# A hybrid decoder block on one core: another order at the start, decay rows stored from ScalarE's queue, and six of the scan's x projections in matmuls of 512 columns

## The chip, the cores and the metric

The kernel runs on one core of a Trainium2 chip. The metric is the device time of one execution in microseconds (us), as a median over runs; lower is better. A profiled execution gives the span from its first to its last instruction, and what each engine did in it: TensorE (PE for matmuls, PEld for loading their stationary operand), VectorE (DVE), ScalarE (ACT), GpSimd (POOL), and SyncE (SP), which here only issues DMAs. SBUF is the on-chip memory; PSUM is the small one into which matmuls accumulate, in banks of 2 KB per partition; 256 tokens of float32 for two column halves fill one bank.

## The reference

One decoder layer, 256 tokens, width 1024, float32. What matters here:

```
proj = rmsnorm(x) @ w_in          # columns: z, xBC, dt, q, k, v, gates
xbc  = silu(causal_dwconv(xBC))   # depthwise, width 4; gives x (2048), B and C (8 groups x 128)
dt   = softplus(dt_raw + bias)    # 32 heads
y    = ssd_scan(x*dt, dt*A, B, C) # chunks of 128; decays exp(cumsum differences)
y    = rmsnorm_by_group((y + x*d) * silu(z)) * w
att  = moba_attention(rope(q), rope(k), v)   # 256 tokens: one causal block
x    = x + (g_ssd*(y@w_ssd) + g_att*(att@w_att)) @ w_out
out  = rmsnorm(x + convffn(rmsnorm(x)))
```

## The kernel before, in words

**Number format.** Every float32 operand of a large matmul is split into a high and a low part (`split_half`: ScalarE copies 128 x 1024 weights into the high part, L107; VectorE subtracts it from the weights, L115). A product is then three matmuls: high by high, high weights by low activations, low weights by high activations. The activations stand as pairs `hn[k]`, high in `[:, 0]` and low in `[:, 1]`, for eight blocks k of 128 input channels.

**Units.** All weights are read in the order of one list (`seq`), 1 MB at a time, through three buffers by SP's queue; `next_unit` loads three units ahead and splits one unit ahead, through four buffers for high halves and four for low ones. A unit of `w_in` is 1024 x 256. `mm_unit` multiplies it in 48 matmuls of 256 columns (L176 to L178), block by block, into one PSUM bank. `mm_wide` uses the pair as one right-hand side of 512 columns (L187: high weights by both parts), then 256 columns for the low weights (L191), into two banks; the part that fell into the second half of each bank is then copied out by ScalarE and added by VectorE.

**Order.** TensorE's order is written by hand. From L302 to L387, the start, the order of ScalarE and VectorE is written by hand too; later a planner orders those two and POOL from the program's order, its own costs and a few `issue_after` marks. Each engine runs its queue strictly in that order, so an instruction that waits holds those behind it.

**The start.** x (transposed) and the first v weights arrive in five pieces (`HEAD`); VectorE weighs x by the norm's weight (L313), ScalarE squares it (L323), TensorE multiplies the raw x for v (L309) and sums the squares (L332). The reciprocal root of the mean comes from ScalarE's Sqrt and VectorE's reciprocal with one Newton step (L339 to L344), is broadcast by a matmul (L260), and multiplies the weighed x (`normed`, L355). The first unit, B and C of group 0, takes its first four blocks as plain float32 (L366, 16 matmuls), since these need no split; its other four go through `mm_unit`.

**The scan, groups g = 0 to 7.** Each group runs `u_bc` (B and C), `u_x`, small matmuls of earlier groups (`small_1`: the scan's output L568, attention scores L608 and outputs L666), `u_qk`, then by turns `u_v`, `u_z`, `u_gate`. `small_2` has the chunk product `s_cb` (L509), the transposes of x (`s_xt`, L537; in groups 2, 4 and 6 by a DMA) and the mean of the gated norm. `conv_silu` runs the width-4 conv: ScalarE starts an accumulator (L398), VectorE adds three shifted products (L402), ScalarE takes a tanh, VectorE multiplies (L406). `u_x` leaves x in its PSUM bank and `u_qk` runs its conv later, straight from the bank, behind the split of the next unit. Four banks go round for all of these (`mm_tile`, tag "mm").

**Decay rows.** `dt_chain` makes dt on small tiles, `dt_sums` the cumulative sums (L705), `dt_turn` transposes them, copies them to SBUF (L716) and stores them to DRAM by POOL's queue (L717). `load_acs(g)` reads four rows back, broadcast to all partitions (L430, POOL's queue); from them ScalarE makes the decays `mx` (L522 to L525), which VectorE multiplies by the chunk product (L527).

**The end.** The down projection's last columns are finished in two token halves: `finished(c, cut)` scales columns up to `cut` on ScalarE and the others on VectorE, and stores both.

Of the kernel before, what the change touches and what calls it, by code (L numbers as in the profile page):

```python
# [19 lines left out]
P = 128  # L20
# [17 lines left out]
C_ID = 256  # L38

HEAD = [0] + [KD + 512 * k for k in (1, 2, 4, 6, 8)]  # L40
# [8 lines left out]
def block_kernel(tc, xtok_d, head_d, par_d, nf_d, con_d, rope_d, win_d, wgate_d, bg_d, watt_d, wssd_d, wout_d, wup_d, wdn_d, out_d):  # L49
# [3 lines left out]
    with st:  # L53
# [11 lines left out]
        con = const.tile([P, C_ID + 7 * P + NH], F32, name="con")  # L65
# [5 lines left out]
        con3 = con[:, C_ID : C_ID + 7 * P].rearrange("p (a b) -> p a b", b=P)  # L71
        ident = con3[:, 0, :]
        mmask = con3[:, 1:4, :]
        amask = con3[:, 4:7, :]
        tri = con3[:, 1, :]
        sel = con[:, C_ID + 7 * P :]
# [5 lines left out]
        nc.scalar.activation(one1, ones[:, 0:1], AF.Sqrt)  # L82
# [73 lines left out]

        def mm_unit(ps, halves, act, first=True, last=True, k0=0, apart=False):


            tiles = [(hi, lo, kk) for hi, lo, n in halves for kk in range(n)]  # L160
            nk = len(tiles)
            km = [(k, m) for k in range(nk) for m in range(2)]
            if apart:
                km.sort(key=lambda x: x[1])
                ps = [p[:, 0, :] for p in ps]
            else:
                ps = [ps[:, m, :] for m in range(2)]
            with tc.manual_schedule(engines=PE_ONLY):
                for k, m in km:
                    hi, lo, kk = tiles[k]  # L170
                    xh, xl = act[k0 + k][:, 0, :], act[k0 + k][:, 1, :]
                    wh = hi[:, kk, m * P : m * P + P]
                    wl = lo[:, kk, m * P : m * P + P]
                    a = first and k == 0 and (m == 0 or apart)
                    z = last and k == nk - 1 and (m == 1 or apart)
                    nc.tensor.matmul(ps[m], wh, xh, start=a, stop=False)  # L176
                    nc.tensor.matmul(ps[m], wh, xl, start=False, stop=False)  # L177
                    nc.tensor.matmul(ps[m], wl, xh, start=False, stop=z)  # L178

        def mm_wide(ps, halves, act, k0=0, nk=KD):  # L180


            tiles = [(hi, lo, kk) for hi, lo, n in halves for kk in range(n)]
            with tc.manual_schedule(engines=PE_ONLY):
                for k, (hi, lo, kk) in enumerate(tiles, k0):
                    for m in range(2):
                        nc.tensor.matmul(flat(ps[m]), hi[:, kk, m * P : m * P + P], flat(act[k]), start=(k == 0),  # L187
                                         stop=False)
                for k, (hi, lo, kk) in enumerate(tiles, k0):
                    for m in range(2):  # L190
                        nc.tensor.matmul(ps[m][:, 1], lo[:, kk, m * P : m * P + P], act[k][:, 0, :], start=False,  # L191
                                         stop=(k == nk - 1))

# [94 lines left out]
        nc.sync.dma_start(con[:, 0 : C_ID + P], con_d[:, 0 : C_ID + P])  # L288
# [3 lines left out]
        nc.sync.dma_start(con[:, C_ID + P :], con_d[:, C_ID + P :])  # L292
        nc.sync.dma_start(rope, rope_d)
        eps = const.tile([P, 1], F32, name="eps")
        n1 = work.tile([P, 4, 2], F32, name="n1")
        rstd1 = n1[:, 3]
# [6 lines left out]
        with tc.manual_schedule(engines=IN_ORDER):  # L303
# [14 lines left out]
            for k in range(2):  # L318
                nc.scalar.activation(sq[:, k], xk[k], AF.Square)
                weigh(k)  # L320
            add(0, 1)
            for k in range(2, KD, 2):
# [8 lines left out]
            for c in range(2):  # L331
                nc.tensor.matmul(stat[:, 0, c : c + 1], sq[:, 0, c * P : c * P + P], ones[:, 0:1], start=(c == 0),  # L332
                                 stop=(c == 1))
            for c in range(2):
                v_raw(6, c)
            v_raw(7, 0)

            mh, root, rr = n1[:, 0], n1[:, 1], n1[:, 2]
            nc.scalar.activation(root, stat[:, 0, 0:2], AF.Sqrt, scale=1.0 / D, bias=eps)  # L339
            nc.vector.tensor_scalar(mh, stat[:, 0, 0:2], -0.5 / D, -0.5 * EPS, op0=ALU.mult, op1=ALU.add)  # L340
            nc.vector.reciprocal(root, root)
# [3 lines left out]
            half0 = split_half(raws[0], 4, 4)  # L345
            rb1 = rms_bcast(rstd1)
            v_raw(7, 1)
            for k in range(KD):
                j = NH * (k % 4)
                nc.tensor.matmul(ps_dt[j : j + NH, 0, :], wdt[:, k], xw[:, k], start=(k < 4), stop=(k >= KD - 4))  # L350

# [11 lines left out]
            for k in range(4):  # L363
                normed(k)
                for m in range(2):
                    nc.tensor.matmul(psbc[:, m], raws[0][:, k, m * P : m * P + P], hnf[k], start=(k == 0 and m == 0),  # L366
                                     stop=False)
            for k in range(4, KD):
                normed(k)
                high(k)  # L370
            for k in range(4, KD):
                low(k)
            nc.scalar.activation(dtp, ps_dt[:, 0, :], AF.Copy)
# [3 lines left out]
            mm_unit(psbc, [half0], hn, first=False, k0=4)  # L377
# [303 lines left out]
        def dt_chain():  # L681
# [18 lines left out]
            nc.vector.tensor_scalar(nega, nega, -1.0, None, op0=ALU.mult)  # L700
            nc.vector.tensor_tensor(r3(3), dt, b3(nega), op=ALU.mult)

        def dt_sums():
# [3 lines left out]
            with tc.high_priority():  # L707
                nc.vector.tensor_copy(flat(acs), ps_a[:, 0, 0 : 2 * NH])
                nc.vector.tensor_tensor(alm, ps_a[:, 0, 2 * NH : 3 * NH], acs[:, 0, :], op=ALU.subtract)

        def dt_turn():
# [3 lines left out]
            with tc.high_priority():  # L715
                nc.scalar.activation(acsT, ps_t[0:NH, 0, :], AF.Copy)  # L716
                nc.gpsimd.dma_start(acsT_d, acsT)  # L717
# [51 lines left out]
        for g in range(NG):  # L769
# [12 lines left out]
            if g % 2 == 0:  # L782
                cols = slice(256 * g, 256 * g + 512)
                for c in range(2):
                    tc.keep_in_program_order(nc.gpsimd.dma_start(gates[:, c, cols], bg_d[cols].partition_broadcast(P)))
# [214 lines left out]
        def finished(c, cut):  # L1000
            lo, hi = xo[:, c, 0:cut], xo[:, c, cut:]
            nc.vector.tensor_scalar(hi, hi, rstd3[:, c : c + 1], None, op0=ALU.mult)
            nc.sync.dma_start(out_d[:, c, cut:], hi)
            nc.scalar.activation(lo, lo, AF.Identity, scale=rstd3[:, c : c + 1])
            (nc.scalar if c else nc.sync).dma_start(out_d[:, c, 0:cut], lo)
# [17 lines left out]
        with tc.manual_schedule(engines=IN_ORDER):  # L1023
# [17 lines left out]
            finished(0, 512)  # L1041
# [10 lines left out]
            finished(1, 352)  # L1052


def _layout(i):
# [48 lines left out]
    con = np.stack([np.eye(P, dtype=np.float32), tri, np.ones((P, P), np.float32), tri, neg, np.zeros((P, P), np.float32), neg], axis=1)  # L1104
# [5 lines left out]
    con = np.concatenate([wdt, con.reshape(P, 7 * P), np.tile(np.eye(NH, dtype=np.float32), (4, 1))], axis=1)  # L1110
# [42 lines left out]
```

## Time and profile before

| | us |
|---|---|
| median of 3 runs | 584.55 (583.65 to 589.18) |
| the profiled execution, its time | 585.26 |
| its span | 583.5 |
| TensorE busy | 572.4 |
| VectorE busy | 457.8 |
| ScalarE busy | 394.8 |
| POOL busy | 66.3 |

Rows of the profile are read so: a row of the timeline has the start in us, the duration in us, engine, line of the kernel, operation, the tiles written and read, and in brackets the engine's idle time before it with what ended that. "x8" are eight of a kind in a row. A row of the chain has start, duration and what. A row of groups has the count, then busy us, the mean in ns of one, the idle time before. A row of DMA issues has KB and the median us from issue to landing. A row of stretches has, for each engine, the busy time and the count, in the order PE, PEld, DVE, ACT, POOL, then clock, share of the DMA engines and GB/s. A row of waits has the total in us, how many, and the longest. A matmul's row is longer than the distance to the next one's start, since matmuls overlap.

### The profile page before, as it was taken

What the parts mean: (1) busy time and instruction counts of PE and PEld (TensorE: products, weight loads), DVE (VectorE), ACT (ScalarE), POOL (GpSimd) and SP (SyncE); (2) the same over time, 40 slices, a digit from 0 to 9 for tenths busy, and PEclk for the clock granted to TensorE, in tenths of its full rate; (3) what the DMA queues carried; (4) which work ended last, traced back from release to release, by engine and by line L of the source; (5) the groups of instructions that cost most, each with busy time, mean ns of one, the idle gap of its engine ahead of it and who ended that gap; (6) DMA issues with size and microseconds to landing.
All of it is one profiled execution on the core that took longest, in us unless ns stands there. A gap on an engine that the chain in (4) does not pass through costs nothing.

```text
span 583.5 us, 9394 instructions
## 1 busy us (share of the span) xinstructions
PE 572.4 (98%) x3510; PEld 502.4 (86%) x3510; DVE 457.8 (78%) x819; ACT 394.8 (68%) x711; POOL 66.3 (11%) x105
## 2 busy tenths in 40 slices
PE   8999989999999999999999999999999999999995
PEld 6899888898988989889888888889888888888884
DVE  4995899889699996998985556768888898884543
ACT  3854698887798777887884344466776767774432
POOL 1001032221223113230121000000000000000200
PEclk9999999999999999999999999999999999999999
DMA  8846556875658946779456756454546555464611
GB/s 304 307 164 244 201 162 210 231 210 188 221 162 195 290 136 220 176 206 292 122 162 240 227 191 214 161 203 144 182 180 216 199 172 206 143 216 155 226 56 72
DMA packets 32845, 113.90 MB, mean 195 GB/s; under 512 B 16880, under 2 KB 17264, under 8 KB 21152
## 3 DMA queue, kind: packets, MB, share of 16 engines
q1 hardware_dynamic: 29632, 104.04, 54.3%
q0 software_dynamic: 2736, 7.51, 4.9%
q10 hardware_dynamic: 432, 1.75, 0.7%
q8 instruction: 27, 0.44, 0.3%
q14 instruction: 18, 0.15, 0.1%
HBM read 108.15 MB, written 1.09 MB: 187 GB/s over the span
## 4 chain that ended last, share of the span: by engine, by line
PE 89%; DMA 3%; DVE 2%; ACT 2%; issue 2%; SPq 0%; POOL 0%; DVEq 0%; ACTq 0%; POOLq 0%
PE up L187 13%; PE mm L208 10%; PE mm L209 10%; PE mm L210 10%; PE mm L187 8%; PE up L191 7%; PE mm L176 6%; PE mm L177 5%; PE mm L178 5%; PE mm L191 4%; PE py L568 2%; DMA raw<-in_win_dram 2%; DMA acsB<-acsT_d 1%; PE po L666 1%; DVE lo L115 1%
## 5 line engine op out<-in xcount | busy, mean ns | idle before, releaser
L115 DVE TENSOR_TENSOR lo<-raw,hi 128x1024 fp32r<-128x1024 f32 x183 | 223.2, 1227 | 69.8 <-ACT hi L107 68.8
L107 ACT ACTIVATE hi<-raw 128x1024 fp32r<-128x1024 f32 x183 | 191.1, 1055 | 105.7 <-PE mm L210 56.3
L176 PE MATMUL mm<-hn,hi 128*128 128x256 f32 x280 | 79.6, 284 | 0.0
L178 PE MATMUL mm<-hn,lo 128*128 128x256 f32 x280 | 79.3, 283 | 0.0
L177 PE MATMUL mm<-hn,hi 128*128 128x256 f32 x280 | 79.2, 283 | 0.0
L187 PE MATMUL up<-xw,hi 128*128 128x512 f32 x320 | 76.3, 391 | 0.0
L187 PEld LDWEIGHTS up<-xw,hi 128*128 128x128 f32 x320 | 58.8, 188 | 11.4
L187 PE MATMUL mm<-hn,hi 128*128 128x512 f32 x224 | 56.8, 395 | 0.0
L177 PEld LDWEIGHTS mm<-hn,hi 128*128 128x128 f32 x280 | 53.7, 192 | 0.2
L176 PEld LDWEIGHTS mm<-hn,hi 128*128 128x128 f32 x280 | 53.7, 192 | 0.2
L178 PEld LDWEIGHTS mm<-hn,lo 128*128 128x128 f32 x280 | 53.7, 192 | 0.1
L402 DVE SCALAR_TENSOR_TENSOR cacc<-mm,par,cacc 128x255 f32<-128x255 f32 (+2 forms) x96 | 44.4, 473 | 3.9 <-ACT cacc L398 3.0
L187 PEld LDWEIGHTS mm<-hn,hi 128*128 128x128 f32 x224 | 40.2, 189 | 8.4 <-issue 1.2
L191 PEld LDWEIGHTS up<-xw,lo 128*128 128x128 f32 x320 | 41.0, 191 | 1.6
L191 PE MATMUL up<-xw,lo 128*128 128x256 f32 x320 | 41.5, 283 | 0.0
L209 PE MATMUL mm<-lo,act 128*128 128x512 f32 (+1 forms) x92 | 35.0, 380 | 0.0
L208 PE MATMUL mm<-hi,act 128*128 128x512 f32 (+1 forms) x92 | 34.9, 380 | 0.0
L210 PE MATMUL mm<-hi,act 128*128 128x512 f32 (+1 forms) x92 | 34.9, 380 | 0.0
L978 POOL TENSOR_TENSOR mt<-x,nfb 128x512 f32<-128x512 f32 x3 | 4.8, 1598 | 258.9 <-DVE x L972 237.6
L191 PEld LDWEIGHTS mm<-hn,lo 128*128 128x128 f32 x224 | 30.6, 190 | 2.2
L191 PE MATMUL mm<-hn,lo 128*128 128x256 f32 x224 | 31.2, 282 | 0.0
L956 DVE SCALAR_TENSOR_TENSOR facc<-ab,par,facc 128x255 f32<-128x255 f32 (+1 forms) x44 | 21.3, 483 | 11.3 <-ACT facc L954 10.6
(226 smaller groups left out, 1130.6 us busy)
## 6 DMA issues: line engine op xcount, KB each, us to landing
raw<-in_win_dram SPq DMA_DIRECT2D x34, 1024.0 KB, 5.9
raw<-in_wup_dram SPq DMA_DIRECT2D x22, 1024.0 KB, 4.8
raw<-in_wdn_dram SPq DMA_DIRECT2D x10, 1024.0 KB, 4.9
raw<-in_wgate_dram SPq DMA_DIRECT2D x8, 1024.0 KB, 5.6
raw<-in_wssd_dram SPq DMA_DIRECT2D x8, 1024.0 KB, 5.1
acsB<-acsT_d POOLq DMA_DIRECT2D x8, 512.0 KB, 5.3
raw<-in_watt_dram SPq DMA_DIRECT2D x4, 1024.0 KB, 5.3
raw<-in_wout_dram SPq DMA_DIRECT2D x4, 1024.0 KB, 5.3
```

The costliest lines, as they stand in the source:

```text
L107: split_half.hi = nc.scalar.activation(hi[:, :n], raw[:, k0 : k0 + n], AF.Copy)
L115: split_half.lo = nc.vector.tensor_tensor(lo[:, :n], raw[:, k0 : k0 + n], hi[:, :n].bitcast(F32), op=ALU.subtract)
L176: nc.tensor.matmul(ps[m], wh, xh, start=a, stop=False)
L177: nc.tensor.matmul(ps[m], wh, xl, start=False, stop=False)
L178: nc.tensor.matmul(ps[m], wl, xh, start=False, stop=z)
L187: nc.tensor.matmul(flat(ps[m]), hi[:, kk, m * P : m * P + P], flat(act[k]), start=(k == 0), stop=False)
L191: nc.tensor.matmul(ps[m][:, 1], lo[:, kk, m * P : m * P + P], act[k][:, 0, :], start=False, stop=(k == nk - 1))
L208: nc.tensor.matmul(o, xh, wh, start=(k == 0 if apart else k0 + k == 0), stop=False)
L209: nc.tensor.matmul(o, xh, wl, start=False, stop=False)
L210: nc.tensor.matmul(o, xl, wh, start=False, stop=(k0 + k == nk - 1))
L402: nc.vector.scalar_tensor_tensor(acc[:, s:], src[:, m, : T - s], w(m, 3 - s), acc[:, s:], op0=ALU.mult, op1=ALU.add)
L956: nc.vector.scalar_tensor_tensor(acc[:, s:], src[:, : T - s], w(2 - s), acc[:, s:], op0=ALU.mult, op1=ALU.add)
```

## The change

- **Start.** x arrives in six pieces (the third is halved) and its first four blocks are squared one at a time; the sums stand before the last raw v product; Abs_reciprocal_sqrt replaces Sqrt and reciprocal; ScalarE's high half of the first unit's second part comes before the broadcast, VectorE's low half only behind the normed rows; the 16 matmuls for dt stand ahead of the broadcast. `mm_passes` runs a unit in passes over all blocks (high by high; low weights by high; high by low for the first unit; both high products, then the low weights, for x of group 0).
- **Small work.** The scalings of `par` and the copy of `acs` go from VectorE to ScalarE; the negation of `nega` is fused; the constants are laid out anew; the loads of the gates' bias (POOL's queue) wait for the start's last split.
- **Decay rows.** Stored by ScalarE's queue.
- **x of groups 2 to 7.** `mm_halves`: for each column half, eight matmuls of 512 columns with the high weights, then eight of 256 with the low weights, into a bank of its own; `joined` copies the second half of each bank out (ScalarE) and adds the first (VectorE) into `xs`; the conv then reads and writes `xs` in SBUF.
- **End.** The second token half in three pieces and three stores.

```diff
-HEAD = [0] + [KD + 512 * k for k in (1, 2, 4, 6, 8)]
+HEAD = [0] + [KD + 512 * k for k in (1, 2, 3, 4, 6, 8)]
...
+        def mm_passes(ps, halves, act, passes, first=True, k0=0):
+            tiles = [(w, kk) for *w, n in halves for kk in range(n)]
+            jobs = [(w, x, k, m) for ws in passes for k in range(len(tiles)) for w, x in ws for m in range(2)]
+            with tc.manual_schedule(engines=PE_ONLY):
+                for i, (w, x, k, m) in enumerate(jobs):
+                    wt, kk = tiles[k]
+                    nc.tensor.matmul(ps[:, m, :], wt[w][:, kk, m * P : m * P + P], act[k0 + k][:, x, :],
+                                     start=first and i == 0, stop=i == len(jobs) - 1)
...
+        def mm_halves(ps, halves, act):
+            tiles = [(hi, lo, kk) for hi, lo, n in halves for kk in range(n)]
+            with tc.manual_schedule(engines=PE_ONLY):
+                for m in range(2):
+                    for k, (hi, lo, kk) in enumerate(tiles):
+                        nc.tensor.matmul(flat(ps[m]), hi[:, kk, m * P : m * P + P], flat(act[k]), start=(k == 0),
+                                         stop=False)
+                    for k, (hi, lo, kk) in enumerate(tiles):
+                        nc.tensor.matmul(ps[m][:, 1], lo[:, kk, m * P : m * P + P], act[k][:, 0, :], start=False,
+                                         stop=(k == KD - 1))
+
+        def joined(dst, ps):
+            for m in range(2):
+                nc.scalar.activation(dst[:, m], ps[m][:, 1], AF.Copy)
+                nc.vector.tensor_tensor(dst[:, m], ps[m][:, 0], dst[:, m], op=ALU.add)
...
-            for k in range(6):
+            for k in range(KD):
                 for c in range(2):
+                    if k == KD - 1 and c:
+                        stats()
                     v_raw(k, c)
...
-            nc.scalar.activation(root, stat[:, 0, 0:2], AF.Sqrt, scale=1.0 / D, bias=eps)
+            nc.scalar.activation(root, stat[:, 0, 0:2], AF.Abs_reciprocal_sqrt, scale=1.0 / D, bias=eps)
-            nc.vector.reciprocal(root, root)
...
-            half0 = split_half(raws[0], 4, 4)
-            rb1 = rms_bcast(rstd1)
-            v_raw(7, 1)
+            hi0 = split_high(raws[0], 4, 4)
             for k in range(KD):
                 j = NH * (k % 4)
                 nc.tensor.matmul(ps_dt[j : j + NH, 0, :], wdt[:, k], xw[:, k], start=(k < 4), stop=(k >= KD - 4))
+            rb1 = rms_bcast(rstd1)
...
+            half0 = split_half(raws[0], 4, 4, hi0)
             for k in range(4, KD):
                 low(k)
...
-            mm_unit(psbc, [half0], hn, first=False, k0=4)
+            mm_passes(psbc, [half0], hn, ([(0, 0)], [(1, 0)], [(0, 1)]), first=False, k0=4)
...
-        with tc.issue_after(hn_end[1]):
+        with tc.issue_after(hn_end[0]):
             for a, b in ((C_NW, C_D), (C_CW, C_FW)):
-                nc.vector.tensor_scalar(par[:, a:b], par[:, a:b], 0.5, None, op0=ALU.mult)
+                nc.scalar.activation(par[:, a:b], par[:, a:b], AF.Copy, scale=0.5)
...
         def u_x(g):
             hv = next_unit()
-            ps = mm_tile()
-            mm_unit(ps, hv, hn)
             xs = S[g]["xs"] = ssp.tile([P, 2, T], F32, tag="xs", bufs=2, name="xs")
-            S[g]["x_ps"] = ps
+            if g > 1:
+                ps = [mm_tile(), mm_tile()]
+                mm_halves(ps, hv, hn)
+                joined(xs, ps)
+                S[g]["x_ps"] = xs
+                return
+            ps = S[g]["x_ps"] = mm_tile()
+            if g:
+                mm_unit(ps, hv, hn)
+            else:
+                mm_passes(ps, hv, hn, ([(0, 0), (0, 1)], [(1, 0)]))
...
-                nc.vector.tensor_copy(flat(acs), ps_a[:, 0, 0 : 2 * NH])
+                nc.scalar.activation(flat(acs), ps_a[:, 0, 0 : 2 * NH], AF.Copy)
...
-                nc.gpsimd.dma_start(acsT_d, acsT)
+                nc.scalar.dma_start(acsT_d, acsT)
...
-                    tc.keep_in_program_order(nc.gpsimd.dma_start(gates[:, c, cols], bg_d[cols].partition_broadcast(P)))
+                    with tc.issue_after(hn_end[1]):
+                        bg = nc.gpsimd.dma_start(gates[:, c, cols], bg_d[cols].partition_broadcast(P))
+                    tc.keep_in_program_order(bg)
...
-            finished(1, 352)
+            finished(1, (0, 256, 640, 1024))
```

More of the change, by code (lines that the diff above doesn't have):

```diff
@@ L64, in block_kernel @@
         par = const.tile([P, NPAR], F32, name="par")
-        con = const.tile([P, C_ID + 7 * P + NH], F32, name="con")
+        con = const.tile([P, C_MASK + 6 * P], F32, name="con")
         rope = const.tile([P, 2, T], F32, name="rope")
@@ L70, in block_kernel @@
         wdt = con[:, 0:C_ID].rearrange("p (k h) -> p k h", h=NH)
[L71 to L76, printed above, removed]
+        ident = con[:, C_ID:C_SEL]
+        sel = con[:, C_SEL:C_MASK]
+        masks = con[:, C_MASK:].rearrange("p (a b) -> p a b", b=P)
+        mmask = masks[:, 0:3, :]
+        amask = masks[:, 3:6, :]
+        tri = masks[:, 0, :]
         ones = const.tile([P, P], F32, name="ones")
@@ L287, in block_kernel @@
             nc.sync.dma_start(head[:, a:b], head_d[P * a : P * b].rearrange("(p n) -> p n", p=P))
-        nc.sync.dma_start(con[:, 0 : C_ID + P], con_d[:, 0 : C_ID + P])
+        nc.sync.dma_start(con[:, 0:C_MASK], con_d[:, 0:C_MASK])
         load_to(1)
@@ L291, in block_kernel @@
         load_to(2)
-        nc.sync.dma_start(con[:, C_ID + P :], con_d[:, C_ID + P :])
+        nc.sync.dma_start(con[:, C_MASK:], con_d[:, C_MASK:])
         nc.sync.dma_start(rope, rope_d)
         eps = const.tile([P, 1], F32, name="eps")
-        n1 = work.tile([P, 4, 2], F32, name="n1")
-        rstd1 = n1[:, 3]
+        mh, root, rr, rstd1 = (work.tile([P, 2], F32, name=n) for n in ("n1mh", "n1r", "n1rr", "rstd1"))
         vt0 = ssp.tile([P, 2, T], F32, tag="vt", bufs=2, name="vt")
@@ L316, in add, with stats @@
                 nc.vector.tensor_tensor(sq[:, a], sq[:, a], sq[:, b], op=ALU.add)
-            for k in range(2):
+            def stats():
+                for c in range(2):
+                    nc.tensor.matmul(stat[:, 0, c : c + 1], sq[:, 0, c * P : c * P + P], ones[:, 0:1], start=(c == 0),
+                                     stop=(c == 1))
+            for k in range(4):
                 nc.scalar.activation(sq[:, k], xk[k], AF.Square)
                 weigh(k)
-            add(0, 1)
-            for k in range(2, KD, 2):
+                if k:
+                    add(0, k)
+            for k in range(4, KD, 2):
                 nc.scalar.activation(sq[:, k : k + 2], chan[:, k : k + 2, 0], AF.Square)
@@ L367, in block_kernel @@
                                      stop=False)
+            nc.scalar.activation(dtp, ps_dt[:, 0, :], AF.Copy)
             for k in range(4, KD):
@@ L699, in dt_chain @@
                 nc.scalar.activation(nega, par[:, C_AL : C_AL + NH], AF.Exp)
-            nc.vector.tensor_scalar(nega, nega, -1.0, None, op0=ALU.mult)
-            nc.vector.tensor_tensor(r3(3), dt, b3(nega), op=ALU.mult)
+            nc.vector.scalar_tensor_tensor(r3(3), dt, -1.0, b3(nega), op0=ALU.mult, op1=ALU.mult)
         def dt_sums():
@@ L998, in rstd_3, with finished @@
             nc.vector.scalar_tensor_tensor(rstd3[:, c : c + 1], h, 1.5, r, op0=ALU.add, op1=ALU.mult)
[L1000 to L1005, printed above, removed]
+        def finished(c, cuts):
+            for i, (a, b) in enumerate(zip(cuts, cuts[1:])):
+                x, r = xo[:, c, a:b], rstd3[:, c : c + 1]
+                if i:
+                    nc.vector.tensor_scalar(x, x, r, None, op0=ALU.mult)
+                else:
+                    nc.scalar.activation(x, x, AF.Identity, scale=r)
+                (nc.sync if i or not c else nc.scalar).dma_start(out_d[:, c, a:b], x)
         ps = [mm_tile(), mm_tile()]
@@ L1040, in block_kernel @@
             rstd_3(0, 1)
-            finished(0, 512)
+            finished(0, (0, 512, 1024))
             add_x3(flat(ps[1])[:, 256:512], 1, 768, 1024)
```

17 lines of the change are left out of this document (6 added, 11 removed).

## The prediction

> **What bounds the kernel now.** I read the page first, then the busy time by stretches, then who waited for whom.
>
> ```profile
> PE 572.4 (98%) x3510; PEld 502.4 (86%) x3510; DVE 457.8 (78%) x819; ACT 394.8 (68%) x711; POOL 66.3 (11%) x105
> ```
>
> ```profile
> 40.00:82.00 42.00, 39.81 (x274) 35.77 (x273) 33.51 (x59) 27.18 (x54) 4.92 (x7) 1.00 0.56 189
> 82.00:300.00 218.00, 217.92 (x1537) 194.66 (x1538) 193.96 (x365) 181.26 (x371) 52.30 (x83) 1.00 0.69 202
> ```
>
> ```profile
> PEld pxt L537 <- DVE xs L406: 2.6, 2, 2.4
> ```
>
> The reader sees a kernel that TensorE bounds: between 82 and 300 us, the scan groups 2 to 7, its matmuls leave 0.08 us of 218 empty. Time can come from three places: the start, before TensorE is in its stream; the one stall inside it, 2.4 us before the transposes L537 of group 1; and fewer or cheaper matmuls. VectorE stands second, with 193.96 of 218 us: whoever gives it work in the scan must ask when TensorE needs what it makes.
>
> All sums below are made against the profiled execution, 585.26 us with a span of 583.5. The median of the runs shown is 584.55, 0.7 us lower, and I take 0.7 off at the end.
>
> **The start.** The norm's mean, its root and its broadcast come one after another, and then VectorE's queue decides.
>
> ```profile
> 13.91 1.22 DVE L115 TENSOR_TENSOR lo<-raw,hi 128x1024 fp32r<-128x1024 f32 x1 [0.70 <-ACT hi L107]
> ```
>
> ```profile
> 14.33 1.07 PE L350 MATMUL ps_dt<-xw,con 128*32 128x256 f32 x16
> 15.05 2.73 DVE L355 TENSOR_TENSOR sq<-xw,pb 128x256 f32<-128x256 f32 x8
> ```
>
> ```profile
> 15.52 3.72 PE L366 MATMUL mm<-sq,raw 128*128 128x256 f32 x16
> ```
>
> ```profile
> 12.46 0.15 DVE L341 RECIPROCAL n<-n 128x2 f32<-128x2 f32 x1
> ```
>
> ```profile
> 13.29 0.68 PE L260 MATMUL pb<-con,n 128*128 128x128 f32 x4
> ```
>
> The broadcast ends at 13.97, but the normed rows (L355) start at 15.05, because the low half of the weights (L115, 1.22 us) stands ahead of them in VectorE's order. The change puts that subtraction behind the eight normed rows, so they start at the broadcast's end. It drops the reciprocal (0.15 us) and puts 16 matmuls of 1.07 us (L350) ahead of the broadcast, into TensorE's wait for the root. The broadcast then ends between 13.8 and 14.0. The first normed row takes 0.34 us (2.73 / 8), so L366 starts near 14.3 in place of 15.52: 1.2 us. The low half comes 2.7 us later than before, and the matmuls now ask for it later: high times high first, then the low weights, then the low activations, three passes of 8 at 0.12 us each. Its eight rows end near 16.6 and the subtraction near 17.8, when L366 ends too (14.3 + 3.72), so nothing new waits. Against a full gain stands the DMA: the first four weight rows must have landed by then, and the two loads of the gate's bias that now wait for the first splits no longer share the engines with them.
>
> ```profile
> 11.05 0.56 POOL L785 DMA_DIRECT2D head<-in_bg_dram  x1 [3.94 <-DVE sq L316]
> ```
>
> One more, smaller load of x at the head lets the first matmuls start sooner, but the last piece, and with it the sum of squares, lands no sooner: the same bytes. The two scalings of par leave VectorE for ScalarE, nega's negation is fused, and the copy of acs leaves VectorE too: four short instructions, at some 0.15 us each by the reciprocal's row, that VectorE no longer has. ScalarE has pauses for its share; if that cover is gone, it costs the same 0.6 us there. I take **-1.3 us**, between 0 (the load of the weights decides) and -2.0 (all of it counts).
>
> **The decay rows and the stall.**
>
> ```profile
> 41.19 0.36 ACT acsT L716
> 41.83 0.52 POOL acsT_d L717
> 42.35 4.82 issue
> 47.19 7.41 DMA acsB<-acsT_d
> ```
>
> ```profile
> 54.63 0.69 ACT L522 ACTIVATE mx<-acsB,acs 128x128 f32<-128x128 f32 x2 [4.73 <-DMA acsB<-acsT_d]
> ```
>
> ```profile
> 58.65 1.23 DVE L115 TENSOR_TENSOR lo<-raw,hi 128x1024 fp32r<-128x1024 f32 x1 [5.34 <-ACT hi L107]
> ```
>
> ScalarE stands 4.73 us for the rows that went to DRAM and back, VectorE 5.34 us behind it; the work that piles up then fills VectorE until the x of group 1 is late, and that is the 2.4 us stall near 79 us. Only the way out changes queue: from POOL to ScalarE's own, directly behind the copy; the way back stays on POOL.
>
> ```profile
> out_dram<-mt ACTq DMA_DIRECT2D x1, 176.0 KB, 2.7
> ...
> acsT_d<-acsT POOLq DMA_DIRECT2D x1, 32.0 KB, 5.1
> ```
>
> No small store on ScalarE's queue under running weight loads is in the trace. Bounds: 5.1 (as now) and 2.7 (ScalarE's store at the end, with the engines empty). The copy-to-issue wait of about 0.3 us goes in any case. So the rows come 0.3 to 2.7 us sooner; I take 2.2, nearer the row of the same queue. VectorE has only short pauses from 61 us to the stall, so a start that much sooner takes as much off: 2.0 of 2.4 us, since TensorE itself also arrives earlier. **-2.0**, ends 0 and -2.4. The price of the issue on ScalarE, about 0.4 us, lies in its wait of 4.73. Late next would be the splits of the following units, which shift along.
>
> [...] The two rows above differ by 2.4 us, though at unlike times.
>
> **The x of groups 2 to 7.** Now 48 matmuls of 256 columns each; then 16 of 512 and 16 of 256.
>
> ```profile
> 20.07 0.28 PE L177 MATMUL mm<-hn,hi 128*128 128x256 f32 x1
> ...
> 22.23 0.28 PE L177 MATMUL mm<-hn,hi 128*128 128x256 f32 x1
> ```
>
> ```profile
> 146.84 1.84 PE mm L187 x8
> 148.68 0.95 PE mm L191 x8
> ```
>
> Between the two L177 rows lie 18 starts: 2.16 / 18 = 0.120 us. Old unit: 48 x 0.120 = 5.76. New, as q and k already run: 2 x (1.84 + 0.95) = 5.58. Gain 0.18 per unit, **-1.1 us** for six. It is small because the columns streamed stay the same; only the pairs grow longer.
>
> What it adds per group are two copies on ScalarE and two additions on VectorE, just as z has them:
>
> ```profile
> 180.91 0.64 ACT L500 ACTIVATE zt<-mm 128x256 f32<-128x256 f32 x2
> ```
>
> ```profile
> 162.45 1.00 DVE L402 SCALAR_TENSOR_TENSOR cacc<-mm,par,cacc 128x255 f32<-128x255 f32 x2 [0.99 <-ACT cacc L398]
> ...
> 167.57 0.47 DVE L402 SCALAR_TENSOR_TENSOR cacc<-mm,par,cacc 128x253 f32<-128x253 f32 x1
> ...
> 181.44 1.22 DVE L115 TENSOR_TENSOR lo<-raw,hi 128x1024 fp32r<-128x1024 f32 x1
> 182.57 0.75 DVE L502 TENSOR_TENSOR zt<-mm,zt 128x256 f32<-128x256 f32 x2
> ...
> 189.28 1.76 DVE L527 TENSOR_TENSOR mx<-mx,cb 128x1536 f32<-128x1536 f32 x1 [0.88 <-ACT mx L525]
> ```
>
> ```profile
> 182.75 0.46 PE L209 MATMUL mm<-lo,hn 128*128 128x512 f32 x1
> ```
>
> ```profile
> L107 ACT ACTIVATE hi<-raw 128x1024 fp32r<-128x1024 f32 x183 | 191.1, 1055 | 105.7 <-PE mm L210 56.3
> ```
>
> 0.64 us on ScalarE is hidden by its pauses. 0.75 us on VectorE is not, in the even groups: from 162.45 to its pause before 189.28 VectorE has no wait worth printing, and the split that started at 181.44 ends at 182.66, 0.09 us before TensorE's L209 needs it at 182.75. The additions for x of group 4 fall into that stretch. TensorE arrives 0.18 sooner, VectorE ends 0.75 later: a stall of 0.75 + 0.18 - 0.09 = 0.84 us. Group 6 repeats group 4 to a tenth:
>
> ```profile
> 252.87 1.22 DVE L115 TENSOR_TENSOR lo<-raw,hi 128x1024 fp32r<-128x1024 f32 x1
> ```
>
> ```profile
> 254.19 0.46 PE L209 MATMUL mm<-lo,hn 128*128 128x512 f32 x1
> ```
>
> For the other four groups, where the same splits end earlier before their use, I take 0.1 together. **+1.8 us.** Ends: 0, if the order of VectorE's queue comes out with the split ahead of other work; and 2.1 for each even group, if VectorE's additions also stand behind a copy and a 1.06 us split (L107) in ScalarE's order (0.75 + 0.32 + 1.06 = 2.1): +6.4.
>
> The second bank of x moves the others on by one: q and k's second bank is now the one that bc of the same group used, so the conv of bc has to be read out before q and k start.
>
> ```profile
> 168.57 2.04 PE mm L187 x8
> ```
>
> Its last step in group 4 ends at 168.04, 0.5 us ahead. Pushed by an addition it would cost some tenths, but out of the same 0.84: TensorE waiting here is no longer early at L209.
>
> [...]
>
> **The end.** The second token half is finished in 256 + 384 + 384 columns with three stores in place of 352 + 672 with two.
>
> ```profile
> 579.02 0.57 DVE L1002 TENSOR_SCALAR mt<-mt,rstd 128x672 f32<-128x672 f32 x1
> ```
>
> The first store can start sooner, but the last one starts behind both VectorE pieces and one more issue on SP's queue: **-0.1**, within 0.3 both ways.
>
> **Sum.** -1.3 - 2.0 - 1.1 + 1.8 - 0.1 = -2.7: 582.6 us as profiled, **581.8** as a median.
>
> **Rivals**, by the median (585.26 + sum - 0.7).
> - *The stall stays*: the store on ScalarE's queue takes its 5.1 us among the weight loads. Speaks for it: the load back on POOL takes 7.41 us there. Sum -0.7: 583.9. Chance 0.20.
> - *The additions cost nothing*: VectorE's order comes out with the weight splits in front; for it, TensorE is not held by any other addition now. Sum -4.5: 580.1. Chance 0.20.
> - *VectorE becomes the bound, slower*: the joins stand behind ScalarE's splits, +6.4 in the even groups. Sum +1.9: 586.5. It turns the sign above 1.5 us for each even group (4.5 / 3), so it needs a wait of 0.7 us besides the additions' own 0.75. Against it: the same pair of copy and addition for q, k and z has no wait worth naming now. Chance 0.13.
> - [...] Chance 0.05. [...]
>
> **Numbers.** The forecast, 580.8 to 582.8, has 0.42. The range takes in the rivals and the ends of the terms: 579.0 to 587.0. About 1% is what a measurement of this kernel tells from no change, since its three runs spread over 5.5 us. Faster by that means below 578.7, which needs every term at its far end: 0.05. Slower, above 590.4, needs the third rival and a start that loses: 0.03. Within: 0.92.
>
> **What would show it.** Right: L366 starts at 14.3 +- 0.3; the wait of ScalarE for acsB is under 3 us and L537 of group 1 waits under 0.6; x of groups 2 to 7 runs in 5.6 us; TensorE waits 0.6 to 1.1 us at L209 of the gate in groups 4 and 6. Wrong: a VectorE pause ahead of the new additions; a wait at the start of q and k of over 0.5 us; L366 held by its weights; or another order of VectorE's queue, which would move every lead quoted here.

## The result, and the profile after

The changed kernel takes **591.29 us** (median of 12 runs, 588.52 to 592.40) against 584.16 us before (12 runs): a ratio of 1.010 [1.0076, 1.0125], slower. Forecast were 581.8 us and a range of 579.0 to 587.0. The profiled execution of after took 589.51 us, its span 587.7: 4.2 us above the span of before. The medians lie 7.1 us apart; the rows below account for the profiled executions, and the last section says why the median one is slower.

Where the time went is read from TensorE's place in its stream: the same matmuls (`py`, the scan's output; `pcb`, the chunk product) in both timelines. Before:

```profile
64.02 0.65 PE L568 MATMUL py<-mx,xt 128*64 128x256 f32 x4
...
93.53 0.65 PE L568 MATMUL py<-mx,xt 128*64 128x256 f32 x4
...
165.40 1.52 PE L568 MATMUL py<-mx,xt 128*64 128x256 f32 x16
...
185.38 0.59 PE L509 MATMUL pcb<-bc 128*128 128x256 f32 x2
...
256.78 0.59 PE L509 MATMUL pcb<-bc 128*128 128x256 f32 x2
```

After:

```profile
63.30 0.65 PE L606 MATMUL py<-mx,xt 128*64 128x256 f32 x4
...
90.03 0.65 PE L606 MATMUL py<-mx,xt 128*64 128x256 f32 x4
...
162.20 1.52 PE L606 MATMUL py<-mx,xt 128*64 128x256 f32 x16
...
184.78 0.59 PE L547 MATMUL pcb<-bc 128*128 128x256 f32 x2
...
260.26 0.59 PE L547 MATMUL pcb<-bc 128*128 128x256 f32 x2
```

Against the kernel before, TensorE is 0.7 us ahead in group 1, 3.5 ahead once the old stall is behind it, 3.2 ahead on entering group 4. In the gate units (`u_gate`) of groups 4 and 6 the lead turns into a lag: 0.6 ahead, then 3.5 behind. The waits of TensorE (total, how many, longest) and its timeline at group 4 say what it waited for:

```profile
PE mm L241 <- DVE lo L117: 5.5, 4, 2.4
```

```profile
176.59 0.39 PE L240 MATMUL mm<-hi,hn 128*128 128x512 f32 x1
179.42 0.50 PE L241 MATMUL mm<-lo,hn 128*128 128x512 f32 x1 [2.44 <-DVE lo L117]
...
250.66 0.39 PE L240 MATMUL mm<-hi,hn 128*128 128x512 f32 x1
253.49 0.79 PE L241 MATMUL mm<-lo,hn 128*128 128x512 f32 x1 [2.44 <-DVE lo L117]
```

The second matmul of the gate wants the low half of its weights. Undisturbed its start follows the first by 0.23 us, here by 2.83: 2.6 us lost, and 2.6 again in group 6. (The idle time in brackets is shorter, since it starts at the end of the first matmul's row. The other two of the four waits, in groups 0 and 2, are 0.4 and 0.2.) VectorE's timeline at group 4 shows why it was late:

```profile
170.74 1.20 DVE L117 TENSOR_TENSOR lo<-raw,hi 128x1024 fp32r<-128x1024 f32 x1
...
171.94 3.57 DVE L432 SCALAR_TENSOR_TENSOR cacc<-xs,par,cacc 128x255 f32<-128x255 f32 x6
175.43 0.74 DVE L482 TENSOR_TENSOR qkraw<-mm,qkraw 128x256 f32<-128x256 f32 x2
176.10 0.74 DVE L436 SCALAR_TENSOR_TENSOR xs<-th,cacc 128x256 f32<-128x256 f32 x2
176.76 0.68 DVE L490 TENSOR_TENSOR qk<-qkraw,rope 128x512 f32<-128x512 f32 x1
177.37 0.86 DVE L633 SCALAR_TENSOR_TENSOR yg<-yg,par,zt 128x256 f32<-128x256 f32 x2
178.16 1.21 DVE L117 TENSOR_TENSOR lo<-raw,hi 128x1024 fp32r<-128x1024 f32 x1
```

In before the same place reads:

```profile
171.39 2.97 DVE L115 TENSOR_TENSOR lo<-raw,hi 128x1024 fp32r<-128x1024 f32 x2
...
174.36 0.46 DVE L402 SCALAR_TENSOR_TENSOR cacc<-mm,par,cacc 128x255 f32<-128x255 f32 x1
174.74 1.21 DVE L115 TENSOR_TENSOR lo<-raw,hi 128x1024 fp32r<-128x1024 f32 x1
175.87 0.47 DVE L402 SCALAR_TENSOR_TENSOR cacc<-mm,par,cacc 128x254 f32<-128x254 f32 x1
```

Two things differ. **The order**: the gate's first low half stood behind the first conv step (174.74 to 175.95; its use was at 180.01) and now stands behind all six, the q and k sums, x, the rotation and the norm. **The duration**: the six conv steps take 3.57 us, where six in a row without a disturbance take 2.4 (a row further down). In before they read x from PSUM (`mm`), here from SBUF (`xs`). At that moment GpSimd copies attention weights in SBUF:

```profile
172.54 1.90 POOL L667 COPY pt<-pr 128x768 uint16<-128x768 uint16 x2 [12.06 <-ACT pr L661]
```

The third loss is the clock. At the end of the wait of group 6 and behind it the stretches (PE, PEld, DVE, ACT, POOL busy, then granted clock) show 0.50 for 3.41 us:

```profile
253.18:256.59 3.41, 3.10 (x7) 2.48 (x8) 3.41 (x8) 0.77 (x3) 0.00 (x0) 0.50 0.62 103
256.59:260.00 3.41, 3.41 (x16) 2.81 (x15) 2.79 (x3) 2.92 (x10) 1.62 (x2) 1.00 0.81 300
```

Its price is read from the same matmuls in both gates: from the late one to `pcb` they take 5.36 us in group 4 (179.42 to 184.78) and 6.77 in group 6 (253.49 to 260.26), 1.4 us more. The account from 3.2 us ahead to 3.5 behind, 6.7 us: 2.6 + 2.6 + 1.4 = 6.6. The 0.4 us that the two x units between the gates should bring aren't seen: at `py` of group 6 TensorE is still 0.55 us ahead (236.28 against 236.83), as behind the gate of group 4.

### The profile page after: what moved, and what is told of

Its sections match the earlier page's. It is cut to its first block, busy times and chain, and to the rows that moved or that the text cites. A ratio compares the mean times of both kernels' runs of the same rounds, so it can differ in the third digit from the quotient of the medians.

```text
span 587.7 us, 9231 instructions
## 1 busy us (share of the span) xinstructions
PE 573.0 (97%) x3414; PEld 498.5 (85%) x3414; DVE 463.0 (79%) x827; ACT 400.1 (68%) x727; POOL 70.2 (12%) x104
## 4 chain that ended last, share of the span: by engine, by line
PE 84%; DVE 10%; ACT 2%; DMA 2%; issue 1%; SPq 0%; POOL 0%; DVEq 0%; ACTq 0%
PE up L200 12%; PE mm L241 10%; PE mm L242 10%; PE mm L240 10%; PE up L204 7%; PE mm L200 4%; PE mm L191 4%; PE mm L189 4%; PE mm L190 4%; PE mm L214 4%; DVE lo L117 3%; DVE cacc L432 3%; PE mm L204 2%; PE mm L217 2%; PE mm L167 1%
## 5 line engine op out<-in xcount | busy, mean ns | idle before, releaser
L200 PEld LDWEIGHTS mm<-hn,hi 128*128 128x128 f32 x224 | 40.2, 189 | 8.4 <-ACT cacc L428 1.2
L191 PE MATMUL mm<-hn,lo 128*128 128x256 f32 x160 | 45.5, 285 | 0.2
L189 PE MATMUL mm<-hn,hi 128*128 128x256 f32 x160 | 45.6, 285 | 0.0
L190 PE MATMUL mm<-hn,hi 128*128 128x256 f32 x160 | 45.3, 283 | 0.0
L204 PEld LDWEIGHTS mm<-hn,lo 128*128 128x128 f32 x224 | 30.6, 190 | 2.2
L241 PE MATMUL mm<-lo,hn 128*128 128x512 f32 x64 | 26.1, 407 | 5.5 <-DVE lo L117 5.5
L204 PE MATMUL mm<-hn,lo 128*128 128x256 f32 x224 | 31.2, 282 | 0.0
L191 PEld LDWEIGHTS mm<-hn,lo 128*128 128x128 f32 x160 | 30.6, 191 | 0.6 <-DVE lo L117 0.6
L190 PEld LDWEIGHTS mm<-hn,hi 128*128 128x128 f32 x160 | 30.6, 191 | 0.2
L189 PEld LDWEIGHTS mm<-hn,hi 128*128 128x128 f32 x160 | 30.6, 191 | 0.2
L432 DVE SCALAR_TENSOR_TENSOR cacc<-mm,par,cacc 128x255 f32<-128x255 f32 (+2 forms) x60 | 27.7, 474 | 3.4 <-ACT cacc L428 3.0
```

What stands on the lines that cost most here:

```text
L241: nc.tensor.matmul(o, xh, wl, start=False, stop=False)
L432: nc.vector.scalar_tensor_tensor(acc[:, s:], src[:, m, : T - s], w(m, 3 - s), acc[:, s:], op0=ALU.mult, op1=ALU.add)
```

## The experiments

Four theories were held against each other. Q: the order of VectorE's queue makes the waits. L: VectorE's load from twelve additions makes them, wherever they stand. W: x, done one column half at a time, holds its weights' buffers to the end, so that later low halves are late. S, formed when the 3.57 us were seen: a conv step with both sources in SBUF is held up by GpSimd's copy. (In the first two expectations S still stands for another rival: that the start or the decay rows cost, and not x.)

### The narrow x back, and the x alone

```diff
-            if g > 1:
+            if g > NG:
```

> The changed kernel with x of groups 2 to 7 back in one bank and 256 columns (the sister). Theory Q (order of VectorE's queue: the join's additions make the planner put the gate's first low half behind the conv of x, and TensorE stands for it in groups 4 and 6): no wait over 0.3 us at the gate's L241 in groups 4 and 6, granted clock 0.998 or more, 3.0 us below the kernel before, 581.2 us. Rival W (weights held longer by the order of a column half at a time): the same. Rival S (the start or the decay rows cost, not x): 587 or more.

583.01 us (582.14 to 583.32), ratio 0.9967 [0.9954, 0.9981]; no wait at the gates of groups 4 and 6. The whole loss hangs on the x. This kernel, all of the change but the wide x, is called the narrow kernel below.

The other way round, the kernel before with `mm_halves`, `joined` and the wide `u_x` alone:

> The kernel before with only the x part. Q: waits of 2 to 2.6 us at the gate in groups 4 and 6, one or two stretches at half clock, less 1.1 us for the matmuls: 589 to 591 us, 5 to 7 above before. W: the same size. S: 583, since x alone saves 1.1 us.

594.45 us, ratio 1.0162 [1.0142, 1.0183]: 2.6 us at each of the same two gates, the old stall (2.2 us at the matmul), and a granted clock of 0.50 for 3.4 us behind all three. Worse than the 589 to 591 forecast, which had one or two such stretches. TensorE is not ahead of the kernel before here, so its earlier arrival is not what makes the waits.

### Matmul order, with and without the wide form

In the changed kernel, block by block:

```diff
-                mm_halves(ps, hv, hn)
+                for i in range(2):
+                    mm_wide(ps, hv[i : i + 1], hn, k0=4 * i)
```

> The changed kernel with the two blocks of k of a wide x one after the other, as q and k are done, in place of one column half after the other: the first block's weights are given back half a unit (2.8 us) earlier, and both banks close at the end. VectorE's order is as in the changed kernel. Theory Q: the waits of 2.4 to 2.6 us at the gate of groups 4 and 6 stay, and so does the time, 588.5 to 592.4 by how many stretches at half clock fall in. Theory W (a column half at a time holds the weights' buffers, and the low halves come late for it): the waits fall to below 0.5 us and the time to 583 to 584.

591.56 us, with the waits as they were. In the narrow kernel, the 48 matmuls sorted by column half:

> e1_narrow (x back in one bank and 48 matmuls of 256 columns) with its matmuls of groups 2 to 7 one column half after the other, so that both blocks of weights are held to the unit's end, without any addition on VectorE and with e1_narrow's order there. Theory Q: 583.0, as e1_narrow, within 0.7 us. Theory W: the low halves behind it are late in each group, 0.3 to 1 us in each of six: 585 to 589.

582.86 us, as the narrow kernel. **W falls on both sides.**

### The gate's splits ahead

Units 14, 25 and 36 are the gate's first in groups 2, 4 and 6.

```diff
+        AHEAD = (14, 25, 36)
...
-                units.append(split_unit(raws[n], seq[n][1]))
+                with tc.high_priority() if n in AHEAD else ExitStack():
+                    units.append(split_unit(raws[n], seq[n][1]))
```

> The changed kernel with the splits of the gate's first unit in groups 2, 4 and 6 given priority, nothing else. Q: the 2.6 us waits go, the clock stays, 6 to 8 us below the changed kernel and 3 to 4 below before: 580.2 to 581.2. Rival L (0.75 us more work per group on VectorE, whatever its order): another low half comes late instead, 0.8 us in each even group, 582 to 583. W: waits stay, since the weights are freed as late as now.

584.10 us (583.37 to 584.64). The 2.6 us are gone, and a smaller wait has come, for another thing:

```profile
178.06 0.50 PE L242 MATMUL mm<-hi,hn 128*128 128x512 f32 x1 [0.78 <-DVE qkraw L484]
```

Since x takes two banks, the gate's second bank is one that q and k used, and their sums now stand behind the conv. So the sums were put ahead too:

```diff
-            for m in range(2):
-                nc.vector.tensor_tensor(raw[:, m], ps[m][:, 0], raw[:, m], op=ALU.add)
+            with tc.high_priority() if g in (2, 4, 6) else ExitStack():
+                for m in range(2):
+                    nc.vector.tensor_tensor(raw[:, m], ps[m][:, 0], raw[:, m], op=ALU.add)
```

> The changed kernel, with the gate's splits of groups 2, 4 and 6 and the sums of q and k of the same groups both put ahead of the convolution in VectorE's queue (e5_gate_ahead moved the splits alone and got a new wait of 0.94 us in each of groups 4 and 6 at the gate's second bank, on the sums of q and k). Theory Q (only the order of VectorE's queue costs time): both kinds of wait are gone, TensorE stands about 4 us ahead of the kernel before at the end of group 6, and the time is 580.5 to 582.5, under e1_narrow's 583.0 by up to 6 x 0.18 us. Theory P (the second bank that the wide form takes turns the rotation of the four banks, so that some bank is late whatever the order): a wait of 0.5 to 1 us moves to another bank, and the time is 583.5 to 584.5, as e5_gate_ahead. Theory L (VectorE's twelve additions cost by their load, wherever they stand): 583.5 to 585, with VectorE late at another place of the even groups.

582.16 us (581.49 to 582.80), ratio 0.9962 [0.9949, 0.9976]: all of the change, all twelve additions, no wait above 0.4 us in groups 4 and 6. L falls as the main cause.

### Load, and order alone

Two plain additions more in each of the narrow kernel's groups 2 to 7; the conv overwrites what they write:

```diff
-            if g:
+            if g > 1:
+                mm_unit(ps, hv, hn)
+                for m in range(2):
+                    nc.vector.tensor_tensor(xs[:, m], ps[:, m], rope[:, m], op=ALU.add)
+            elif g:
```

> The sister (e1) with two more additions of 128 x 256 on VectorE per group 2 to 7, from x's bank and the rope table into xs, where the conv overwrites them: the output doesn't change, the matmuls don't either. Q: the gate's low half again stands behind the conv, TensorE waits 2 us or more in groups 4 and 6, 586 to 588 us. L: waits of 0.75 us, 582.7 us. W: no wait, as e1, 581.2 us.

585.06 us, between the theories: a wait of 0.98 us in each of groups 4 and 6. Its timeline shows that the planner, given these additions, put the low half behind the conv here as well (the last step at 176.00, the low half at 177.18). So load and order are not independent: the load is what moves the order. The order without any load is had by an `issue_after` in the narrow kernel, the gate's first low half of groups 4 and 6 behind the conv's last product:

> e1_narrow (x in one bank, no additions) with one thing moved in VectorE's queue: the first low half of the gate of groups 4 and 6 stands behind the conv, as in the changed kernel, in place of ahead of its second step. From e1_narrow's trace the low half would start 1.1 us before 177.5 and end near 177.6, against TensorE's need at 177.23: a wait of 0.3 to 0.6 us in each of the two groups, 583.0 + 0.8 = 583.8 (583.4 to 584.4). That is the price of the order without the additions (0.75 us per group) and without the conv steps that last 1.04 in place of 0.47 us in the changed kernel (two per group). Theory Q in its simple form (the order alone costs the waits): 2.4 us each, 588 or above.

585.40 us, ratio 1.0003 [0.9983, 1.0023]. The interval of the two starts is 1.14 us where 0.23 is undisturbed:

```profile
176.73 0.39 PE L245 MATMUL mm<-hi,hn 128*128 128x512 f32 x1
177.87 0.50 PE L246 MATMUL mm<-lo,hn 128*128 128x512 f32 x1 [0.75 <-DVE lo L118]
```

0.9 us, more than the 0.3 to 0.6 expected, and far from 2.4. The order is one part.

### The wide x in groups without a gate

```diff
-            if g > 1:
+            if g in (3, 5, 7):
```

> The changed kernel with the wide x in groups 3, 5 and 7 alone, which have no gate behind q and k; groups 2, 4 and 6 are as in the kernel before, and so is VectorE's order in them. Theory Q: no wait at the gate in groups 4 and 6, three units 0.18 us shorter each: 583.0 - 0.5 = 582.5 (582.0 to 583.0). Theory L: half of the additions are left, and with e7_narrow_load's 2.05 us for twelve plain additions half of that is lost: 584.0. If the wide form by itself costs in TensorE's queue (a bank awaited at the next unit), 584 to 586, with that wait in groups 3, 5 and 7.

582.71 us, ratio 0.9968 [0.9948, 0.9988]: no wait at the gates of groups 4 and 6. In these groups the wide form is harmless; three units' 0.5 us isn't told apart from the narrow kernel.

### GpSimd's copies

x's sum written back to PSUM, so that the conv reads it there:

```diff
-                nc.vector.tensor_tensor(dst[:, m], ps[m][:, 0], dst[:, m], op=ALU.add)
+                nc.vector.tensor_tensor(ps[m][:, 0], ps[m][:, 0], dst[:, m], op=ALU.add)
...
-                S[g]["x_ps"] = xs
+                S[g]["x_ps"] = [p[:, 0] for p in ps]
```

once with the low half held where the changed kernel has it, once free:

> The changed kernel with the sum of x written back into its PSUM bank, so that the conv reads it there and not from SBUF, and with the first low half of the gate of groups 4 and 6 held behind the same work of VectorE as in the changed kernel. Theory S (two conv steps per group last 1.04 in place of 0.47 us because GpSimd copies in SBUF at the same time, and a step with one source in PSUM is not touched by that): all steps last 0.47 us, the low half comes 1.1 us sooner, the waits at the gate of groups 4 and 6 fall from 2.4-2.6 to 1.3-1.5 us, and the time is 585.5 to 587.0. If the slow steps have another reason, they stay at 1.04 us, the waits at 2.4 us, the time at 588.5 or above. If x's two banks, now held through the conv, make z or the gate wait, a new wait shows there and takes the gain.

> As e17_psum_same_order, but with VectorE's order left to the planner: the gate's first low half of groups 4 and 6 then stands ahead of the rotation of q and k and of the norm's products, 1.4 us of work sooner. Theory S with Q: low half ready near the need, waits of 0 to 0.3 us, 581.5 to 583.0. If the two banks held through the conv cost: 0.3 to 1 us in each group at z, 584 to 588.

595.78 and 595.76 us: both slower, by the new wait that the expectations named as a rival, and by more than the 584 to 588 given for it. x's two banks, held through the conv, make z wait, three times in each kernel, 8.6 us in all:

```profile
177.26 1.19 PE L205 MATMUL mm<-hn,hi 128*128 128x512 f32 x2 [2.94 <-DVE cacc L437]
```

But the steps themselves answered. With PSUM as a source (the view of one tile; ns least, median, most):

```profile
L437 DVE SCALAR_TENSOR_TENSOR cacc<-mm,par,cacc x6: 461/470/474, 175.1 to 177.0; 128x255 f32<-128x255 f32 x2, 128x254 f32<-128x254 f32 x2, 128x253 f32<-128x253 f32 x2
```

though GpSimd copied beside most of them:

```profile
175.70 1.60 POOL L672 COPY pt<-pr 128x768 uint16<-128x768 uint16 x2 [12.49 <-ACT pr L666]
```

and in the changed kernel, from SBUF:

```profile
L432 DVE SCALAR_TENSOR_TENSOR cacc<-xs,par,cacc x6: 465/474/1043, 171.9 to 175.0; 128x255 f32<-128x255 f32 x2, 128x254 f32<-128x254 f32 x2, 128x253 f32<-128x253 f32 x2
```

Not every step beside a copy is slow: of these six two are, as in each of groups 3 to 7. The trace of before had the sign already. There only the conv's last product (L406) reads twice from SBUF, and four of its sixteen lasted 0.90 to 1.05 us, where the other twelve lasted 0.41 to 0.43; each of the four stood beside a copy:

```profile
141.73 1.05 DVE L406 SCALAR_TENSOR_TENSOR xs<-th,cacc 128x256 f32<-128x256 f32 x1
```

```profile
141.29 1.21 POOL L629 COPY pt<-pr 128x768 uint16<-128x768 uint16 x1 [1.30 <-ACT pr L623]
```

For its price, the overlap alone is taken away. A one-column copy on GpSimd that reads the gate's low half stands ahead of its copies in groups 4 and 6; VectorE's order is that of the changed kernel (`a_p` holds GpSimd's copies and the transposes behind them):

```diff
+                if g in (4, 6):
+                    with tc.issue_after(nc.gpsimd.tensor_copy(seen, units[-1][0][1][:, 0, 0:1].bitcast(F32)).ins):
+                        a_p(g - 1)
```

> The changed kernel with GpSimd's copies of the attention weights in groups 4 and 6 held until the gate's first low half is done, so that they no longer run beside the conv. VectorE's order is that of the changed kernel. Theory S (two sources in SBUF wait for GpSimd's copy): the six conv steps last 0.47 us each in groups 4 and 6, 2 x 0.57 = 1.1 us less ahead of the low half, and the waits at the gate fall from 2.4-2.6 to 1.3-1.5 us: 588.5 - 2.2 = 586.3 (585.5 to 587.5), plus up to 1.9 for each stretch at half clock. If the order alone makes the waits, they stay at 2.4-2.6 us: 588.5 to 592.4. The copies then run beside later work of VectorE; if that costs as much, the time stays too, with the wait at another place.

586.44 us (585.94 to 587.10), as S said. The six steps, VectorE's low half and TensorE's wait:

```profile
172.25 2.44 DVE L432 SCALAR_TENSOR_TENSOR cacc<-xs,par,cacc 128x255 f32<-128x255 f32 x6
...
177.38 1.22 DVE L117 TENSOR_TENSOR lo<-raw,hi 128x1024 fp32r<-128x1024 f32 x1
```

```profile
176.90 0.39 PE L240 MATMUL mm<-hi,hn 128*128 128x512 f32 x1
178.65 0.50 PE L241 MATMUL mm<-lo,hn 128*128 128x512 f32 x1 [1.36 <-DVE lo L117]
```

1.75 - 0.23 = 1.5 us are left of 2.6. So each wait, if the parts add up, is **0.9 order** (the narrow kernel with the order alone), **1.1 GpSimd's copies** (2.6 - 1.5), and 0.6 for the rest. The rest is seen in VectorE's place: it reaches the conv 4.9 us ahead of TensorE's need in the changed kernel (171.94 to 176.82) and 5.7 in the narrow one with the order alone (171.30 to 176.96), 0.8 later, of which it makes up 0.2 on the way to the low half once the copies are away. That is the size of the two additions, 0.75, but that they are its cause isn't shown: with plain additions in the narrow kernel it is still 5.6 us ahead (171.93 to 177.48), and the wait is 0.98, hardly more than the order's.

The rows agree with S: up to 1043 ns from SBUF beside a copy, 474 at most from PSUM beside one, and GpSimd's two copies are the longer as well, 1.90 us against 1.60. By what means the one holds up the other isn't shown.

### The decay rows, the start and the end apart

```diff
-                nc.gpsimd.dma_start(acsT_d, acsT)
+                nc.scalar.dma_start(acsT_d, acsT)
```

in the kernel before, with nothing else:

> The kernel before with one edit: the decay rows are stored by ScalarE's queue. VectorE's order is the same. By the prediction's term (-2.0, ends 0 and -2.4): 584.6 - 2.0 = 582.6, with ScalarE's wait for the rows under 3 us and no stall of 2.4 us at the transposes of group 1. Then the start and the end of the change are left with the rest of e1_narrow's gain, 0 to 0.5 us. If instead the start's earlier arrival is what takes the stall away, the stall stays here and the time is 584 or above.

582.52 us (581.67 to 583.75), ratio 0.9953 [0.9934, 0.9972], no stall at group 1. All that the narrow kernel gained is here already. The end as it was, in the narrow kernel:

> e1_narrow (decay rows and start as changed, x in one bank) with the end as before, two stores for the second token half in place of three. From the traces the last matmul to the end takes 6.64-6.7 us with two and 7.05-7.08 with three: 583.0 - 0.4 = 582.6. What is then left under e12_decay_alone's 582.5 is the start: by the traces' 0.3 us at the scan's end it would be 582.2 to 582.6.

582.35 us (582.18 to 582.76), ratio 0.9957 [0.9942, 0.9973]. By the ratios the end's third store costs 0.6 us, though their intervals overlap, and the start brings nothing that the times tell from the decay rows alone.

### The fastest version

All of the change, the gate's splits and the q and k sums ahead, the old end:

> e8_ahead_qk (all of the change, with the gate's splits and the sums of q and k ahead of the conv in groups 2, 4 and 6) with the end as before. 582.2 - 0.4 = 581.8 (581.2 to 582.4), the fastest of the series; if the end's stores cost nothing in the time, 582.2.

**581.74 us** (581.16 to 582.21), ratio 0.9946 [0.9928, 0.9964], against 582.35 (582.18 to 582.76) for the narrow x with the same end, measured together: of the 1.1 us that the wide x was to bring by its matmuls, 0.6, once VectorE's order is set by hand.

## Why the prediction was wrong, and where it was right

**The step that failed is the VectorE term of the x, +1.8.** It put 0.75 us of additions into VectorE's queue as it stood in before, and had 0.84 us at L209. The waits came at the place and in the groups named, and were 2.6 us each; in the profile the term was 5.2 us, and 6.6 with the clock behind the second. Two assumptions carried it. First, that the order would stay: the lead of 0.09 us was read at the second half's matmul, 182.75, while the first half, which was done four microseconds early, was not asked about; the planner moved just that one. The prediction named another order as what would prove it wrong, and gave it no price. Second, that a conv step costs the same from SBUF as from PSUM: `xs` in place of the bank made it 0.57 us longer beside GpSimd's copy (1.04 in place of 0.47), twice in each of groups 3 to 7 and once in group 2. GpSimd's 52 us of work between 82 and 300 stood in the forecast's own row of stretches and was asked nothing. Measured apart, the order is 0.9 of each 2.6 us and the copies 1.1; where the last 0.6 come from is open.

The rival that the additions cost nothing had its condition right: with the order set by hand they cost nearly nothing, though 582.2 us is above its 580.1, by the start's gain that is missing and the end. The slower rival had the right sign and the wrong mechanism: the copies do stand behind splits on ScalarE (L223 at 161.13, behind two that start at 159.24), but VectorE reaches the additions only at 164.14, without a pause ahead of them. The bank of q and k, forecast to cost some tenths, cost none in the changed kernel; when the gate alone was put ahead, the gate's second bank waited 0.9 us on their sums.

**The decay rows, -2.0: right.** Alone they bring 1.9 by the medians (584.46 to 582.52). Against those runs of before whose mean clock was 0.996 or more (14 of 23) it is 1.4; the last section says what the others may be. By the prediction's own signs: the store took 1.5 us (DMA issues: KB, median us to landing), 3.6 less than in before (5.1) and less than the lower bound of 2.7, and ScalarE waits no more.

```profile
acsT_d<-acsT ACTq DMA_DIRECT2D x1, 32.0 KB, 1.5
```

```profile
48.06 1.06 ACT L109 ACTIVATE hi<-raw 128x1024 fp32r<-128x1024 f32 x1 [1.65 <-PE mm L242]
49.02 0.68 ACT L560 ACTIVATE mx<-acsB,acs 128x128 f32<-128x128 f32 x2
```

**The start, -1.3: right at its place, mis-sized in the sum.** The plain float32 matmuls begin at 14.35, forecast 14.3. That is the earliest of fourteen traces with this start; the others have 14.52 to 15.29; the three with the old start have 15.27 to 15.81. So the sign is right, and that this profile hits the forecast so closely is luck.

```profile
14.35 0.92 PE L395 MATMUL mm<-sq,raw 128*128 128x256 f32 x3 [0.51 <-DVE sq L384]
...
39.81 0.50 PE L241 MATMUL mm<-lo,hn 128*128 128x512 f32 x1 [0.43 <-DVE lo L117]
```

But TensorE then reaches the gate of group 0 before its low half, and 0.7 us of the 1.2 go there (0.91 between starts, 0.23 undisturbed). What a start saves is worth only what the next late instruction leaves. Of the rest the traces show 0.4 us at the last matmul, 573.85 in the narrow kernel with the old end against 574.22 with the decay rows alone; the times don't tell the two apart.

**The x's matmuls, 0.18 a unit: right.** One column half to the next is 2.79 us, forecast 1.84 + 0.95:

```profile
156.53 2.00 PE L214 MATMUL mm<-hn,hi 128*128 128x512 f32 x8
...
159.32 2.00 PE L214 MATMUL mm<-hn,hi 128*128 128x512 f32 x8
```

**The end, -0.1 within 0.3: wrong by 0.5.** From the start of the last matmul to the end the trace has 7.06 us, before 6.70; every kernel with three stores has 7.05 to 7.08, every one with two 6.55 to 6.71. The two kernels given the old end ran 0.4 and 0.7 us under theirs with the new one. SP issues twice in a row where it issued once:

```profile
583.41 0.81 SPq L1046 DMA_DIRECT2D out_dram<-mt  x2
```

The prediction had seen that issue and not charged it.

## What to carry to other kernels

When an edit adds work to an engine whose order a planner makes, price the orders that could come out, not only the work: the safest-looking instruction can be the one that moves. Moving an operand from PSUM to SBUF can make an instruction of VectorE read twice from SBUF: look for GpSimd work beside it (here two of six conv steps took 1.04 us in place of 0.47). A slower result with a clear late instruction is worth more runs with that instruction put ahead, and then the next late one: here 1% slower became level with before (584.10 us), then 0.4% faster, and 0.5% with the old end.

## What the chip showed that was not expected

A wait of TensorE of 2.2 to 2.9 us could cost more than itself: from 1.0 us before its end to 1.8 us behind it the granted clock fell to 0.50 for 3.41 us. In the changed kernel's profile that came with one of two equal waits; with the blocks in turn, with both; with the x alone, with all three; with x's sum in PSUM, with two of three (one of them 6.83 us long) and with three of three. The waits of 1.5 us and less in the scan were followed by none, and so was the stall in the profile of before. The runs of the changed kernel fall into heaps that fit none, one and two such stretches: 588.5 us at a mean clock of 0.998, 589.5 to 590.8 at 0.994 to 0.995, 591.8 to 592.4 at 0.991 to 0.992. That is most of its spread, and the profiled execution is of the middle heap. The kernel before has such runs too: of the 23 measured beside the decay rows alone, 9 had a mean clock of 0.994 or less and took 585.4 to 589.3 us, where none of the 12 without the stall was under 0.996. So its stall may have cost some runs a stretch as well; no trace of one was kept.

With the x alone the stretches start at 82.60, 185.00 and 260.09 us, 102.40 and 75.09 apart: 30.0 and 22.0 times their length of 3.41 us. By these three starts, an estimate, they stand on a fixed beat; whether a wait costs one would then depend on where in it the wait falls, which no run tested.
